# A fixed TensorE order for the first stage of a two-layer backbone, with the spread sums left in PSUM

## The chip, the cores and the metric

The kernel runs on one core of a Trainium2 chip. The metric is the device time of one execution in microseconds; lower is better. A core has five engines with their own instruction queues: TensorE (PE in the profile; PEld is its weight loads), VectorE (DVE), ScalarE (ACT), GpSimd (POOL) and SyncE (SP), which issues the DMAs here. Engines wait for each other through semaphores, each in the order of its own queue.

## The reference

512 latent tokens and 256 context tokens of width 1024 pass through two layers. Each normalizes its tokens, scales and shifts them by a vector computed from a condition, applies a mixer, and adds the result through a gate. The part that matters here is the head of layer 0: the norm, the modulation, and the first product with `w_in`.

```python
D_MODEL, SEQ, CTX_LEN, DEPTH = 1024, 512, 256, 2

def _rms(x):
    xf = x.astype(F32)
    return xf * lax.rsqrt(jnp.mean(xf * xf, axis=-1, keepdims=True) + NORM_EPS)

def modulation(cond, mod_w, mod_b):
    m = jax.nn.silu(cond) @ mod_w + mod_b
    return jnp.split(m, 3, axis=-1)

def trunk_layer(x, ctx, c, c_ctx, mod_w, mod_b, norm_g, mixer, need_ctx_out):
    sh, sc, gt = modulation(c[:, None, :], mod_w, mod_b)
    shc, scc, gtc = modulation(c_ctx, mod_w, mod_b)
    h = rmsnorm(x, norm_g) * (1.0 + sc) + sh
    hc = rmsnorm(ctx, norm_g) * (1.0 + scc) + shc
    y, yc = mixer(h, hc, need_ctx_out)        # layer 0 starts with u = h @ w_in, uc = hc @ w_in
    x = x + gt * y
    if need_ctx_out:
        ctx = ctx + gtc * yc
    return x, ctx
...
    for i in range(DEPTH):                    # layer 0: gated linear recurrence, layer 1: retention
        mod_w, mod_b, norm_g, mixer = layers[i]
        x, ctx = trunk_layer(x, ctx, c, c_ctx, mod_w, mod_b, norm_g, mixer, i < DEPTH - 1)
    return rmsnorm(x, final_norm_g)
```

## The kernel before

All 768 tokens are held transposed: 8 chunks of 128 features on partitions (k = 0 to 7), tokens in the free dimension, 256 context tokens first (`acc_c`), then 512 latent ones (`acc_l`). Each float32 product is three fp32r products: every operand is split into a high part and the rest (`hh`, `hl` for the input, `whi`, `wlo` for the weights), and `mm3` (lines 76 to 78) issues whi x hl, whi x hh and wlo x hh. The tiles of a tile framework are recorded in program order; a scheduler sets the order on each engine, and `tc.issue_after` holds an instruction behind another one. The framework adds the semaphore waits. PSUM is four tiles `slots[0]` to `slots[3]` of 1024 columns.

The first stage, lines 244 to 381, goes from x to the first three column tiles of `h @ w_in`:

- x, 3 MB, comes in eight loads on SP; behind them stand, alternating, tiles of `w_in` (`wraw`, 512 KB) and of the modulation weights (`mraw`, 1 MB for each chunk).
- 48 matmuls of ones (`warm_up`) stand on TensorE while x arrives. ScalarE squares x (lines 306 and 307) and VectorE adds the squares up in `ssum` (line 309).
- `token_sums` (line 198) sums over partitions with six matmuls of one column, line 204 and 205 take square root and reciprocal, `token_spread` (line 209) spreads the result over all partitions with six matmuls, and line 319 copies it to `rstd` in SBUF. `normed(k)` (lines 348 and 349) multiplies a chunk with it: `nx`.
- `mod_mm(f)` (line 328) is the modulation product of a chunk, 16 matmuls of 128 columns; the result is copied to `rows` (line 332). `mod_out(f)` sums it with one selection matmul (line 172) and makes `m` (line 338) and `g` (line 343). The banks are `slots[3][:, 0:512]` and `[:, 512:1024]` in turn.
- `make_h` (lines 223 to 228) scales and shifts `nx` and splits it into `hh` and `hl`.
- For each chunk, `mm_in` then runs three units of six matmuls of 384 columns, one for each weight tile, into slots 0, 1 and 2. The next chunk's modulation product stands ahead of them, its selection matmul behind the first unit.

Behind the stage 16 iterations, the mixer's second half and layer 1 follow; they are not changed.

## Time and profile before

| | us |
|---|---|
| median of 3 runs | 1084.09 |
| lowest, highest | 1082.47, 1084.88 |
| the profiled execution | 1081.4 |
| its span | 1079.6 |
| TensorE busy | 1055.1 (98%) |
| VectorE busy | 707.0 (65%) |
| ScalarE busy | 573.2 (53%) |

The profile is one execution, and its rows are read against its own time. A busy engine at 98% says that little can be hidden and that its idle times are the ones to look for; where they are, the windows and waits by stage say. A matmul in float32 is shown as two, so that a count of x12 stands for six.

### The profile page before, as it was taken

What the parts mean: (1) busy time and instruction counts of PE and PEld (TensorE: products, weight loads), DVE (VectorE), ACT (ScalarE), POOL (GpSimd) and SP (SyncE); (2) the same over time, 40 slices, a digit from 0 to 9 for tenths busy, and PEclk for the clock granted to TensorE, in tenths of its full rate; (3) what the DMA queues carried; (4) which work ended last, traced back from release to release, by engine and by line L of the source; (5) the groups of instructions that cost most, each with busy time, mean ns of one, the idle gap of its engine ahead of it and who ended that gap; (6) DMA issues with size and microseconds to landing.
All of it is one profiled execution on the core that took longest, in us unless ns stands there. A gap on an engine that the chain in (4) does not pass through costs nothing.

```text
span 1079.6 us, 13986 instructions
## 1 busy us (share of the span) xinstructions
PE 1055.1 (98%) x5708; PEld 931.9 (86%) x5708; DVE 707.0 (65%) x991; ACT 573.2 (53%) x745; POOL 1.1 (0%) x5
## 2 busy tenths in 40 slices
PE   8999999999999999999999999999999999999996
PEld 8897879999999999998887778888888888887886
DVE  5776767886688687879989746444554535643356
ACT  6567768767687468788365443123431334322344
POOL 0000000000000000000000000000000000000000
PEclk9999999999999999999999999999999999999998
DMA  9524552221122121222114412212123021220202
GB/s 365 219 88 160 194 176 95 69 85 53 69 69 69 49 69 41 78 77 77 62 40 146 163 43 72 85 39 79 40 78 98 20 78 58 79 99 0 79 1 79
DMA packets 29041, 95.48 MB, mean 88 GB/s; under 512 B 2993, under 2 KB 6193, under 8 KB 27953
## 3 DMA queue, kind: packets, MB, share of 16 engines
q1 hardware_dynamic: 28976, 94.59, 25.3%
q8 instruction: 44, 0.72, 0.3%
q14 instruction: 21, 0.16, 0.0%
HBM read 92.48 MB, written 2.10 MB: 88 GB/s over the span
## 4 chain that ended last, share of the span: by engine, by line
PE 62%; DVE 7%; ACT 7%; issue 2%; DVEq 0%
PE ps L76 21%; PE ps L77 20%; PE ps L78 20%; ACT g L468 1%; ACT a L467 1%; DVE xl L264 1%; DVE g L486 1%; ACT q L470 1%; ACT L483 1%; ACT L467 1%; ACT g L452 1%; DVE wlo L92 1%; DVE q L499 1%; DVE q L492 1%; DVE q L498 1%
## 5 line engine op out<-in xcount | busy, mean ns | idle before, releaser
L76 PE MATMUL ps<-hl,whi 128*128 128x384 f32 (+2 forms) x816 | 286.2, 352 | 1.6 <-DVE hl L228 1.3
L78 PE MATMUL ps<-hh,wlo 128*128 128x384 f32 (+2 forms) x816 | 283.1, 347 | 0.1
L77 PE MATMUL ps<-hh,whi 128*128 128x384 f32 (+2 forms) x816 | 283.0, 347 | 0.0
L91 ACT ACTIVATE whi<-wraw 128x1024 fp32r<-128x1024 f32 (+1 forms) x125 | 125.1, 1002 | 212.8 <-PE ps L77 176.0
L92 DVE TENSOR_TENSOR wlo<-wraw,whi 128x1024 fp32r<-128x1024 f32 (+1 forms) x126 | 145.1, 1153 | 95.5 <-ACT whi L91 79.0
L76 PEld LDWEIGHTS ps<-hl,whi 128*128 128x128 f32 x816 | 153.4, 188 | 20.2 <-issue 4.3
L78 PEld LDWEIGHTS ps<-hh,wlo 128*128 128x128 f32 x816 | 153.4, 188 | 11.0 <-issue 0.8
L77 PEld LDWEIGHTS ps<-hh,whi 128*128 128x128 f32 x816 | 153.5, 188 | 10.2 <-issue 1.0
L76 PE MATMUL ps<-yl,whi 128*128 128x384 f32 (+2 forms) x416 | 142.8, 345 | 3.9 <-DVE yl L501 2.0
L77 PE MATMUL ps<-yh,whi 128*128 128x384 f32 (+2 forms) x416 | 142.2, 342 | 0.0
L78 PE MATMUL ps<-yh,wlo 128*128 128x384 f32 (+2 forms) x416 | 141.2, 342 | 0.0
L76 PEld LDWEIGHTS ps<-yl,whi 128*128 128x128 f32 x416 | 78.0, 188 | 12.8 <-DVE yl L501 2.9
L78 PEld LDWEIGHTS ps<-yh,wlo 128*128 128x128 f32 x416 | 78.2, 188 | 5.5
L77 PEld LDWEIGHTS ps<-yh,whi 128*128 128x128 f32 x416 | 78.2, 188 | 5.0
L76 PE MATMUL ps<-wlo,hh 128*128 128x512 f32 x192 | 75.0, 394 | 1.6 <-DVE rb L673 1.6
L77 PE MATMUL ps<-whi,hh 128*128 128x512 f32 x192 | 74.8, 390 | 0.0
L78 PE MATMUL ps<-whi,hl 128*128 128x512 f32 x192 | 74.3, 389 | 0.0
L452 ACT ACTIVATE g<-ps,vt 128x768 f32<-128x768 f32 x64 | 56.1, 897 | 8.9 <-PE ps L78 8.8
L264 DVE SCALAR_TENSOR_TENSOR xl<-ps,vt,xl 128x255 f32<-128x255 f32 (+1 forms) x96 | 54.3, 605 | 0.0
L630 DVE TENSOR_TENSOR vl<-ps,vh 128x512 fp32r<-128x512 f32 x24 | 16.4, 689 | 49.0 <-ACT vh L629 49.0
L76 PE MATMUL ps<-xlo,whi 128*128 128x384 f32 x128 | 44.5, 349 | 4.0 <-DVE xl L264 2.2
L629 ACT ACTIVATE vh<-ps 128x512 fp32r<-128x512 f32 x24 | 14.1, 598 | 62.0 <-PE ps L78 62.0
(190 smaller groups left out, 1585.6 us busy)
## 6 DMA issues: line engine op xcount, KB each, us to landing
wraw<-in_ret_w_in_dram SPq DMA_DIRECT2D x48, 512.0 KB, 3.5
wraw<-in_lru_w_in_dram SPq DMA_DIRECT2D x32, 512.0 KB, 3.8
mraw<-in_lru_mod_sc_dram SPq DMA_DIRECT2D x8, 1024.0 KB, 10.5
wraw<-in_ret_mod_w_dram SPq DMA_DIRECT2D x16, 512.0 KB, 4.8
wraw<-in_lru_w_out_dram SPq DMA_DIRECT2D x16, 512.0 KB, 3.4
wraw<-in_ret_w_out_dram SPq DMA_DIRECT2D x16, 512.0 KB, 3.9
wraw<-in_lru_w_g_dram SPq DMA_DIRECT2D x16, 256.0 KB, 2.7
wraw<-in_lru_mod_gt_dram SPq DMA_DIRECT2D x8, 512.0 KB, 4.0
```

Source lines behind the costliest of these rows:

```text
L76: nc.tensor.matmul(ps, lhsT=lhs[0], rhs=rhs[1], start=first, stop=False)
L77: nc.tensor.matmul(ps, lhsT=lhs[0], rhs=rhs[0], start=False, stop=False)
L78: return nc.tensor.matmul(ps, lhsT=lhs[1], rhs=rhs[0], start=False, stop=last)
L91: nc.scalar.activation(out=hi, in_=raw, func=AF.Copy)
L92: nc.vector.tensor_tensor(out=lo, in0=raw, in1=hi.bitcast(F32), op=ALU.subtract)
L264: nc.vector.scalar_tensor_tensor(out=t[:, o0:o1], in0=u[:, o0 + sh:o1 + sh], scalar=cw[j], in1=t[:, o0:o1], op0=ALU.mult, op1=ALU.add)
L452: nc.scalar.activation(out=t, in_=ps[:, 128:896], func=AF.Sigmoid, bias=vt[:, boff:boff + 1])
L467: nc.scalar.activation(out=a, in_=r, func=AF.Exp, scale=sneg[:, d * CT + c:d * CT + c + 1])
L468: nc.scalar.activation(out=r, in_=r, func=AF.Tanh, scale=spos[:, d * CT + c:d * CT + c + 1])
L470: nc.scalar.activation(out=q, in_=a, func=AF.Square)
L629: nc.scalar.activation(out=hi, in_=src, func=AF.Copy)
L630: nc.vector.tensor_tensor(out=lo, in0=src, in1=hi.bitcast(F32), op=ALU.subtract)
```

## The change

Loads: the last pair of x loads changes places, the first modulation tile is loaded ahead of the first weights, and four modulation tiles are asked for ahead. The table for the square root is loaded on ScalarE right behind the first activation. The sums: six chunks are squared and added as before, the last two are squared by both engines and go to TensorE as separate matmuls that accumulate in the same six columns, behind a matmul with zeros that opens the accumulation. Square root and reciprocal are taken once for all six columns. The spread is written to `slots[3][:, 256:512]` and `[:, 512:1024]` and read there by `normed`, without the copy to `rstd`; the modulation products use columns 0 to 128 and 128 to 256 of the same slot. The first three weight tiles are split in two parts, the first 128 columns and the rest (`w_part`). Every TensorE instruction of the stage is tied to the one recorded before it (`pin`). From the third chunk on, modulation products stand two chunks ahead of their units.

```diff
-            nc.sync.dma_start(out=acc_c[:, k:k + 2, :], in_=xv[:, k:k + 2, 0:NC])
-            nc.sync.dma_start(out=acc_l[:, k:k + 2, :], in_=xv[:, k:k + 2, NC:NT])
-        nc.scalar.activation(out=cond[:, :, 0:2], in_=vt[:, V_COND:V_COND + 16].rearrange("p (k t) -> p k t", t=2),
+            for a, sl in ((acc_c, slice(0, NC)), (acc_l, slice(NC, NT)))[::-1 if k == 6 else 1]:
+                nc.sync.dma_start(out=a[:, k:k + 2, :], in_=xv[:, k:k + 2, sl])
+        silu = nc.scalar.activation(out=cond[:, :, 0:2], in_=vt[:, V_COND:V_COND + 16].rearrange("p (k t) -> p k t", t=2),
                              func=AF.Silu)
+        with tc.issue_after(silu.ins):
+            nc.scalar.activation(out=warm, in_=eps, func=AF.Sqrt)
...
+            mraw = {0: mod_load(0)}
             fetch_to(0)
-            mraw = {0: mod_load(0)}
-            fetch_to(1)
             mraw[1] = mod_load(1)
             fetch_to(2)
-            mraw[2] = mod_load(2)
+            mraw[2], mraw[3] = mod_load(2), mod_load(3)
...
+            def pin(fn, *args):
+                with ExitStack() as st:
+                    if last_pe[0] is not None:
+                        st.enter_context(tc.issue_after(last_pe[0].ins))
+                    last_pe[0] = fn(*args)
...
-            warm_up(48)
+                    m = nc.tensor.matmul(slots[2][:, 0:P], lhsT=ones, rhs=ones, start=True, stop=True)
+                return m
...
+            def sums_of(parts, first, last):
+                for n, (sq, t) in enumerate(parts):
+                    m = nc.tensor.matmul(tok[:, t:t + 1], lhsT=sq[:, t * P:(t + 1) * P], rhs=ones[:, 0:1], start=False,
+                                         stop=last and n == len(parts) - 1)
+                return m
+
+            tok = slots[1][:, 0:6]
+            none = mp1.tile([P, 6], F32, name="none")
+            nc.vector.memset(none, 0.0)
+            pin(warm_up, 46)
...
-            for k in range(KD):
+            for k in range(6):
...
-            rstd = mp1.tile([P, NT], F32, name="rstd")
-            parts = [(ssum[:, a:b], slots[1][:, 512 * i:512 * i + 4], (slots[0], slots[2])[i][:, 512:512 + b - a], rstd[:, a:b], b - a)
-                     for i, (a, b) in enumerate(segs)]
-            for sq, pt, _, _, n in parts:
-                token_sums(pt, sq, n)
-            warm_up(2)
-            rts = [token_rstd(pt, n, D)[0] for _, pt, _, _, n in parts]
-            for rt, (_, _, ps, rs, n) in zip(rts, parts):
-                spread = token_spread(ps, rt, n)
-                nc.scalar.activation(out=rs, in_=ps, func=AF.Copy)
-
-            bank = [slots[3][:, 0:512], slots[3][:, 512:1024]]
+            sq6, sq7 = e("sq6"), e("sq7")
+            for k, sq in ((6, sq6), (7, sq7)):
+                nc.scalar.activation(out=sq[:, NC:NT], in_=acc_l[:, k, :], func=AF.Square)
+                nc.vector.tensor_tensor(out=sq[:, 0:NC], in0=acc_c[:, k, :], in1=acc_c[:, k, :], op=ALU.mult)
+            nc.vector.tensor_tensor(out=sq6[:, NC:NT], in0=sq6[:, NC:NT], in1=sq7[:, NC:NT], op=ALU.add)
+            pin(lambda: nc.tensor.matmul(tok, lhsT=ones, rhs=none, start=True, stop=False))
+            pin(sums_of, [(ssum, t) for t in range(6)], True, False)
+            pin(sums_of, [(sq, t) for sq in (sq6, sq7) for t in range(2)], False, False)
+            pin(sums_of, [(sq6, t) for t in range(2, 6)], False, True)
+            rt = mp1.tile([P, 6], F32, name="rt6")
+            nc.scalar.activation(out=rt, in_=tok, func=AF.Sqrt, scale=1.0 / D, bias=eps)
+            nc.vector.reciprocal(out=rt, in_=rt)
+            rsp = [slots[3][:, 256:512], slots[3][:, 512:1024]]
...
+                bank = slots[3][:, P * (f % 2):P * (f % 2) + P]
...
+                if f + 4 < KD:
+                    mraw[f + 4] = mod_load(f + 4)
+                rows[f] = mp.tile([P, P], F32, tag="rows", name="rows", bufs=2)
+                nc.scalar.activation(out=rows[f], in_=bank, func=AF.Copy)
+                return m
+
+            def mod_out(f):
+                pt = slots[3][:, P * (f % 2):P * (f % 2) + 4]
...
-                nc.vector.tensor_tensor(out=t[:, 0:NC], in0=acc_c[:, k, :], in1=rstd[:, 0:NC], op=ALU.mult)
-                nc.vector.tensor_tensor(out=t[:, NC:NT], in0=acc_l[:, k, :], in1=rstd[:, NC:NT], op=ALU.mult)
+                nc.vector.tensor_tensor(out=t[:, 0:NC], in0=acc_c[:, k, :], in1=rsp[0], op=ALU.mult)
+                nc.vector.tensor_tensor(out=t[:, NC:NT], in0=acc_l[:, k, :], in1=rsp[1], op=ALU.mult)
...
+            def w_part(i, sl):
+                if i == len(w3):
+                    w3.append((wp.tile([P, 1024], F32R, tag="whi", name="whi"), wp.tile([P, 1024], F32R, tag="wlo", name="wlo")))
+                raw, (hi, lo) = raws[i][0], w3[i]
+                nc.scalar.activation(out=hi[:, sl], in_=raw[:, sl], func=AF.Copy)
+                nc.vector.tensor_tensor(out=lo[:, sl], in0=raw[:, sl], in1=hi[:, sl].bitcast(F32), op=ALU.subtract)
...
+            head, rest = slice(0, P), slice(P, 1024)
+            us[0], gps, us[1] = slots[0], slots[1], slots[2]
+            dst = [us[0], gps, us[1]]
+
+            def unit(k, i):
+                return mm_in(w3[i], dst[i], [k])
...
+            pin(mod_mm, 0)
+            pin(token_spread, rsp[0], rt[:, 0:2], NC)
+            pin(token_spread, rsp[1], rt[:, 2:6], NL)
+            w_part(0, head)
+            nx = normed(0)
+            pin(mod_out, 0)
+            make_hs(0, nx)
+            pin(warm_up, 3)
+            pin(mod_mm, 1)
+            pin(warm_up, 2)
+            with tc.issue_after(last_lo[0].ins):
+                nx = normed(1)
+                w_part(1, head)
+                w_part(0, rest)
+            pin(unit, 0, 0)
+            pin(mod_out, 1)
+            make_hs(1, nx)
+            w_part(2, head)
+            with tc.issue_after(last_lo[0].ins), tc.issue_after(last_hi[0].ins):
+                nx = normed(2)
+                w_part(1, rest)
+                w_part(2, rest)
+            pin(unit, 0, 1)
+            pin(unit, 0, 2)
+            pin(mod_mm, 2)
+            pin(unit, 1, 0)
+            pin(mod_out, 2)
+            make_hs(2, nx)
+            nx = normed(3)
+            pin(unit, 1, 1)
+            pin(unit, 1, 2)
+            pin(mod_mm, 3)
+            pin(unit, 2, 0)
+            pin(mod_out, 3)
+            make_hs(3, nx)
+            nx = normed(4)
+            pin(unit, 2, 1)
+            pin(mod_mm, 4)
+            pin(unit, 2, 2)
+            pin(mod_out, 4)
...
+                if k + 2 < KD:
+                    pin(mod_mm, k + 2)
+                pin(unit, k, 0)
+                if k + 2 < KD:
+                    pin(mod_out, k + 2)
+                    make_hs(k + 2, nx)
                     if k + 3 < KD:
-                        mraw[k + 3] = mod_load(k + 3)
-                    rows = mod_mm(k + 1)
-                    nx = normed(k + 1)
-                mm_in(w3[0], us[0], [k])
-                if k + 1 < KD:
-                    mod_out(k + 1, rows)
-                mm_in(w3[1], gps, [k])
-                mm_in(w3[2], us[1], [k])
+                        nx = normed(k + 3)
+                pin(unit, k, 1)
+                pin(unit, k, 2)
```

On TensorE, from the program's start to the first product: `ones` are warm-up matmuls, `ssum` and `sq` token sums, `rt` the spread, `mraw` a modulation product, `rows` a selection, `ps_67` to `ps_70` slots 0 to 3. Before:

```order
L300 MATMUL ps_69<-ones 128x128 x50
L198 MATMUL ps_68<-ones,ssum 128x1 x6
L209 MATMUL ps_67<-vt,rt 128x128 x2
L209 MATMUL ps_69<-vt,rt 128x128 x4
L328 MATMUL ps_70<-mraw,cond 32x128 x16
L300 MATMUL ps_69<-ones 128x128 x2
L172 MATMUL ps_70<-vt,rows 128x4
```

The same place in the changed program:

```order
L311 MATMUL ps_69<-ones 128x128 x46
L336 MATMUL ps_68<-none,ones 128x6
L316 MATMUL ps_68<-ones,ssum 128x1 x6
L316 MATMUL ps_68<-ones,sq_196 128x1 x2
L316 MATMUL ps_68<-ones,sq_197 128x1 x2
L316 MATMUL ps_68<-ones,sq_196 128x1 x4
L351 MATMUL ps_70<-mraw,cond 32x128 x16
L209 MATMUL ps_70<-vt,rt_218 128x128 x6
L362 MATMUL ps_70<-vt,rows 128x4
```

The modulation product of chunk 0 now stands ahead of the spread, and the spread writes slot 3.

On TensorE, from the last unit of chunk 0 to the first of chunk 1, with the semaphores that an instruction waits for (DMAHW of a load, DVE_49 of VectorE, Activation_49 of ScalarE). Before:

```order
L78 MATMUL ps_69<-hh,wlo 128x384
L328 MATMUL ps_70<-mraw,cond 32x128 [waits DMAHW6_49]
L328 MATMUL ps_70<-mraw,cond 32x128 x15
L76 MATMUL ps_67<-hl,whi 128x384 [waits DVE_49]
L77 MATMUL ps_67<-hh,whi 128x384 [waits Activation_49]
```

The same place in the changed program:

```order
L78 MATMUL ps_69<-hh,wlo 128x384
L351 MATMUL ps_70<-mraw,cond 32x128 [waits DMAHW6_49,DVE_49]
L351 MATMUL ps_70<-mraw,cond 32x128 x15
L76 MATMUL ps_67<-hl,whi 128x384
L77 MATMUL ps_67<-hh,whi 128x384 [waits Activation_49]
```

The wait for VectorE has moved from the unit to the modulation product of chunk 2.

On VectorE, around hl of chunk 1 (`hl`) and nx of chunk 2 (`nx`). Before:

```order
L225 TENSOR_SCALAR tmp<-nx,g_82,m_81 128x256 [waits DVE_49]
L348 TENSOR_TENSOR nx<-acc_c,rstd 128x256
L228 TENSOR_TENSOR hl<-tmp,hh 128x256 [waits DVE_49,Activation_49]
L349 TENSOR_TENSOR nx<-acc_l,rstd 128x512 [waits DMAHW4_49]
L228 TENSOR_TENSOR hl<-tmp,hh 128x512 [waits Activation_49]
L338 TENSOR_TENSOR m_81<-ps_70,vt 128x2x2 [waits PE_49]
```

The same place in the changed program:

```order
L225 TENSOR_SCALAR tmp<-nx,g_82,m_81 128x256 [waits DVE_49]
L228 TENSOR_TENSOR hl<-tmp,hh 128x256 [waits DVE_49,Activation_49]
L228 TENSOR_TENSOR hl<-tmp,hh 128x512 [waits Activation_49]
L374 TENSOR_TENSOR nx<-acc_c,ps_70 128x256 [waits DMAHW3_49]
L375 TENSOR_TENSOR nx<-acc_l,ps_70 128x512
L385 TENSOR_TENSOR wlo<-wraw,whi 128x896 [waits Activation_49] x2
L363 TENSOR_TENSOR m_81<-ps_70,vt 128x2x2 [waits PE_49]
```

nx of chunk 2 has moved behind both parts of hl of chunk 1 and reads slot 3; two weight rests stand between it and m of chunk 2.

## Rows read from the trace of the kernel before

**Rows 1.** the windows by stage; columns: window, its length, busy us of each engine with instructions, granted clock, DMA share, GB/s

```profile
15.50:23.67 8.17, 6.46 (x98) 5.67 (x98) 5.14 (x13) 4.70 (x10) 0.00 (x0) 1.00 1.02 418
23.67:59.70 36.03, 35.00 (x351) 31.26 (x352) 24.85 (x74) 20.32 (x35) 0.00 (x0) 1.00 0.53 203
```

**Rows 2.** the timeline to the first product; start us, us, engine, line, operation, idle before

```profile
13.97 1.17 PE L300 MATMUL ps<-ones 128*128 128x128 f32 x9
...
15.53 1.50 PE L198 MATMUL ps<-ones,ssum 128*128 128x1 f32 x12 [0.38 <-DVE ssum L309]
...
17.58 1.60 PE L209 MATMUL ps<-vt,rt 128*128 128x128 f32 x12 [0.56 <-DVE rt L205]
...
19.11 1.08 PE L328 MATMUL ps<-mraw,cond 128*32 128x128 f32 x32
...
19.85 0.69 DVE L349 TENSOR_TENSOR nx<-acc_l,rstd 128x512 f32<-128x512 f32 x1 [0.68 <-ACT rstd L319]
...
20.26 0.28 ACT L332 ACTIVATE rows<-ps 128x128 f32<-128x128 f32 x1 [0.44 <-PE ps L328]
...
21.01 0.16 DVE L338 TENSOR_TENSOR m<-ps,vt 128x4 f32<-128x4 f32 x1 [0.47 <-PE ps L172]
...
22.93 0.69 DVE L228 TENSOR_TENSOR hl<-tmp,hh 128x512 fp32r<-128x512 f32 x1
...
23.67 0.45 PE L76 MATMUL ps<-hl,whi 128*128 128x384 f32 x1 [1.14 <-DVE hl L228]
```

**Rows 3.** waits of the weight loads, 23.6 to 60 us; waiter, waited for: total, times, longest

```profile
PEld ps L76 <- DVE hl L228: 3.2, 6, 1.4
...
PEld ps L172 <- ACT rows L332: 0.7, 1, 0.7
PEld ps L78 <- DVE wlo L92: 0.6, 2, 0.5
```

**Rows 4.** the timeline from selection matmul to nx, chunks 2 and 5

```profile
30.22 0.28 PE L172 MATMUL ps<-vt,rows 128*128 128x4 f32 x2
...
32.00 0.68 DVE L349 TENSOR_TENSOR nx<-acc_l,rstd 128x512 f32<-128x512 f32 x1
...
43.55 0.38 PE L172 MATMUL ps<-vt,rows 128*128 128x4 f32 x2 [0.40 <-ACT rows L332]
...
45.75 0.68 DVE L349 TENSOR_TENSOR nx<-acc_l,rstd 128x512 f32<-128x512 f32 x1
```

**Rows 5.** the timeline around chunk 1 and the third modulation product

```profile
24.14 1.22 DVE L92 TENSOR_TENSOR wlo<-wraw,whi 128x1024 fp32r<-128x1024 f32 x1
...
25.73 1.31 ACT L223 ACTIVATE hh<-nx,m,g 128x256 fp32r<-128x256 f32 x2 [0.89 <-DVE g L343]
...
26.94 0.80 ACT L227 ACTIVATE tmp<-nx,m,g 128x512 f32<-128x512 f32 x1
...
27.78 1.08 PE L328 MATMUL ps<-mraw,cond 128*32 128x128 f32 x32
```

**Rows 6.** the timeline of one unit between product and selection

```profile
48.15 0.44 PE L76 MATMUL ps<-hl,whi 128*128 128x384 f32 x1
...
49.31 0.28 PE L172 MATMUL ps<-vt,rows 128*128 128x4 f32 x2
```

**Rows 7.** the timeline of VectorE, two 768-column operations with and without a PSUM source

```profile
64.37 0.96 DVE L277 TENSOR_TENSOR sil<-ps,sil 128x768 f32<-128x768 f32 x1
...
68.00 0.96 DVE L271 TENSOR_TENSOR xlo<-xl,xh 128x768 fp32r<-128x768 f32 x1
```

**Rows 8.** TensorE's timeline at two long idle times, and a window at the end

```profile
520.87 0.50 PE L76 MATMUL ps<-yl,whi 128*128 128x512 f32 x1 [1.71 <-DVE yl L501]
...
1070.75 0.61 PE L198 MATMUL ps<-ones,fs 128*128 128x1 f32 x4 [1.96 <-DVE fs L851]
...
1072.00:1074.00 2.00, 1.23 (x4) 0.93 (x4) 0.72 (x2) 0.00 (x0) 0.00 (x0) 0.50 0.87 285
```

**Rows 9.** TensorE's waits from 60 to 480 us

```profile
PE ps L182 <- DMA wraw<-in_ret_mod_w_dram: 1.2, 1, 1.2
```

More of the change, by code (lines that the diff above doesn't have):

```diff
@@ L282, in mm_in @@
                 for a, b in halves:
-                    mm3(ps[:, 128 + a:128 + b], wk, cut(hs[k], a, b), k == 0, k == KD - 1)
+                    m = mm3(ps[:, 128 + a:128 + b], wk, cut(hs[k], a, b), k == 0, k == KD - 1)
+            return m
         with tc.tile_pool(name="mp", bufs=4) as mp, tc.tile_pool(name="mp1", bufs=1) as mp1:
@@ L289, in mod_load @@
                 return t
+            mraw = {0: mod_load(0)}
             fetch_to(0)
-            mraw = {0: mod_load(0)}
-            fetch_to(1)
             mraw[1] = mod_load(1)
             fetch_to(2)
-            mraw[2] = mod_load(2)
+            mraw[2], mraw[3] = mod_load(2), mod_load(3)
+            rows = {}
+            last_pe = [None]
+            def pin(fn, *args):
[3 more added lines that the diff above has]
+                    last_pe[0] = fn(*args)
             def warm_up(n):
                 for _ in range(n):
-                    nc.tensor.matmul(slots[2][:, 0:P], lhsT=ones, rhs=ones, start=True, stop=True)
-            warm_up(48)
+                    m = nc.tensor.matmul(slots[2][:, 0:P], lhsT=ones, rhs=ones, start=True, stop=True)
[9 more added lines that the diff above has]
+            pin(warm_up, 46)
             ssum = e("ssum")
-            for k in range(KD):
+            for k in range(6):
                 sq = ssum if k == 0 else e("sq")
@@ L327, in mod_mm @@
                         j = 2 * s + k % 2
-                        nc.tensor.matmul(bank[f % 2][32 * j:32 * j + 32, 0:P], lhsT=cond[:, k, :],
-                                         rhs=raw[:, (s * KD + k) * P:(s * KD + k + 1) * P],
-                                         start=(k < 2), stop=(k >= KD - 2), tile_position=(0, 32 * j))
-                rows = mp.tile([P, P], F32, tag="rows", name="rows", bufs=2)
-                nc.scalar.activation(out=rows, in_=bank[f % 2][:, 0:P], func=AF.Copy)
-                return rows
-            def mod_out(f, rows):
-                pt = bank[f % 2][:, 128:132]
-                mod_sum(rows, slice(0, P), V_SEL, 4, pt)
+                        m = nc.tensor.matmul(bank[32 * j:32 * j + 32, :], lhsT=cond[:, k, :],
+                                             rhs=raw[:, (s * KD + k) * P:(s * KD + k + 1) * P],
+                                             start=(k < 2), stop=(k >= KD - 2), tile_position=(0, 32 * j))
+                if f + 4 < KD:
+                    mraw[f + 4] = mod_load(f + 4)
+                rows[f] = mp.tile([P, P], F32, tag="rows", name="rows", bufs=2)
+                nc.scalar.activation(out=rows[f], in_=bank, func=AF.Copy)
+                return m
+            def mod_out(f):
+                pt = slots[3][:, P * (f % 2):P * (f % 2) + 4]
+                m = nc.tensor.matmul(pt, lhsT=rows[f], rhs=vt[:, V_SEL:V_SEL + 4], start=True, stop=True)
                 nc.vector.tensor_tensor(
@@ L344, in mod_out, with make_hs @@
                                                scalar2=vt[:, V_LG + f:V_LG + f + 1], op0=ALU.add, op1=ALU.mult)
+                return m
             def normed(k):
                 t = e("nx")
-                nc.vector.tensor_tensor(out=t[:, 0:NC], in0=acc_c[:, k, :], in1=rstd[:, 0:NC], op=ALU.mult)
-                nc.vector.tensor_tensor(out=t[:, NC:NT], in0=acc_l[:, k, :], in1=rstd[:, NC:NT], op=ALU.mult)
-                return t
-            split_to(0)
-            with tc.issue_after(spread.ins):
-                rows = mod_mm(0)
-            mod_out(0, rows)
-            warm_up(4)
-            us[0], gps, us[1] = slots[0], slots[1], slots[2]
-            nx = normed(0)
-            for k in range(KD):
+                nc.vector.tensor_tensor(out=t[:, 0:NC], in0=acc_c[:, k, :], in1=rsp[0], op=ALU.mult)
+                nc.vector.tensor_tensor(out=t[:, NC:NT], in0=acc_l[:, k, :], in1=rsp[1], op=ALU.mult)
+                return t
+            w3 = []
+            def w_part(i, sl):
[4 more added lines that the diff above has]
+                nc.vector.tensor_tensor(out=lo[:, sl], in0=raw[:, sl], in1=hi[:, sl].bitcast(F32), op=ALU.subtract)
+            def make_hs(k, nx):
                 tmp = e("tmp")
@@ L363, in backbone @@
                 make_h(cut(hs[k], NC, NT), NL, nx[:, NC:NT], g0[:, k, 0:1], m0[:, k, 0:1], tmp[:, NC:NT], k == 0)
-                if k == 0:
-                    with tc.issue_after(last_lo[0].ins), tc.issue_after(last_hi[0].ins):
-                        w3 = take(3, 2)
+            head, rest = slice(0, P), slice(P, 1024)
[43 more added lines that the diff above has]
+            pin(mod_out, 4)
+            make_hs(4, nx)
+            nx = normed(5)
+            for k in range(3, KD):
                 if k == 3:
```

4 lines of the change are left out of this document (3 added, 1 removed).

## The prediction

> **What bounds the kernel now.** I read the windows by stage first: from the first product to the end of the first stage (23.67 to 59.70 us) TensorE is busy 35.00 of 36.03 us, at a granted clock of 1.00, while VectorE and ScalarE are far from full [rows 1]. What counts is where TensorE stands still. Then the timeline ahead of the first product, read backwards [rows 2]: the product at 23.67 waited for hl, which hangs on m (21.01), on the modulation product (19.11) and on nx, which ends at 19.85 + 0.69 = 20.54; nx hangs on the spread matmuls (17.58), these on the token sums (15.53). So the chain from x is the bound until 23.67. Last the waits of the weight loads from there to the end of the stage [rows 3]: 3.2 us for hl, of which 1.4 stand ahead of the first product, 0.7 for rows, 0.6 for wlo, together 1.8 + 0.7 + 0.6 = 3.1 us of holes. The whole prize is these 3.1 us and whatever the chain gives ahead of 23.67. Behind the stage the order of every engine is the same in both programs, so a shift of its end shifts the whole.
>
> **The chain, step by step.** *Warm-up and sums.* Nine warm-up passes span 1.17 us from 13.97, so with 0.28 for the last one a pass is issued every 0.11 [rows 2]. The new order has 46 warm-up matmuls before the sums where the old had 50, two passes each: 8 passes or 0.89 us less, so TensorE is free at about 14.98 - 0.89 = 14.09 instead of waiting for ssum until 15.53. But the sums are now 1 + 6 + 4 + 4 = 15 matmuls or 30 passes where they were 12 (1.50 us). 29 x 0.111 + 0.25 = 3.48, so they end at 17.57, against 15.53 + 1.50 = 17.03. Their data are no limit, since the last one is wanted only at 16.6 and the old, longer chain of adds was done at 15.5. **+0.5 us.**
>
> *Modulation product and spread.* The product of chunk 0 now stands ahead of the spread: it starts 0.2 behind the last sum's last pass (17.52) and ends 1.08 later, at 18.60 [rows 2]. Square root and reciprocal run beside it; 17.58 - 17.03 = 0.55 puts them at 18.1. The spread, however, writes columns 256 to 512 of slot 3, and the product and its copy use columns 0 to 128. The built order makes the spread wait for ScalarE, and the value that it waits for is that of the copy to rows. The copy takes 0.28 [rows 2]: 18.60 + 0.07 + 0.28 + 0.05 = 19.00 against 17.58. The copy of the sums to rstd is saved, yet nx now waits for all twelve passes (1.60, so 20.65) and runs 0.33 + 0.69 to 21.67, against 20.54. The selection matmul waits for nx, which reads the same bank: it starts at 21.72, m at 22.14 against 21.01. From m to the first product took 23.67 - 21.01 = 2.66; 0.08 of it goes, since the next nx no longer stands in between. First product at about 24.7: **+1.05 us** instead of a gain. If the first modulation load is late, up to 19.11 - 17.5 = 1.6 is added; I take nothing, because it moves ahead of a 512 KB load, 1.3 us at 418 GB/s [rows 1].
>
> *Reading the sums from PSUM.* No row has nx with such a source. The nearest are two 768-column tensor_tensor, one with a PSUM source and one without, both 0.96 [rows 7]. I take no extra cost; as bounds I put 0 and 0.06 on each of some fourteen reads in the chain, under 1 us.
>
> **The stage.** From chunk 2 on, the product of a chunk waits not only for its load but for VectorE, as the built order shows, and by the value of the wait it is the 512-column nx of the same chunk. Before, nx read rstd from SBUF and nobody waited for it. So each modulation product now stands behind a VectorE chain, and in the pinned order no unit can pass it. A product takes 1.08 [rows 5], a unit of six matmuls 1.16 behind a product (48.15 to 49.31) and 1.04 behind another unit, the selection 0.23 with the slower start behind it [rows 6].
>
> *Chunk 2.* hl of chunk 0 starts at 24.7 - 0.74 = 23.96 (22.93 to 23.67 before [rows 2]). Behind it stand on VectorE its own 0.60, nx(1) with 0.33 + 0.60, a weight head of 128 columns, 0.2, the rest of the first weight, 1.0 (896 columns at the rate of the 1.22 for 1024 [rows 5]), then m, the second head and g, 0.6: tmp and hh of chunk 1 start at 27.3. To the end of tmp it took 26.94 + 0.80 - 25.73 = 2.01 [rows 5]; hl 0.60 and nx(2) 0.33 + 0.69 follow: 30.95, and 0.05 for the wait. TensorE is done with three units and a selection at 24.7 + 0.1 + 3.12 + 0.23 = 28.15. Hole **2.85 us**; the product stands at 31.0 where it stood at 27.78 [rows 5].
>
> *Chunks 3 to 7.* From the selection to the end of the next nx took 32.00 + 0.68 - 30.22 = 2.46 us in an order on VectorE that is kept; with softplus steps between, 45.75 + 0.68 - 43.55 = 2.88 [rows 4]. With 0.05 for the wait, and as cover the selection and the units in between: chunk 3 has two units (0.23 + 2.08), hole 0.2; chunk 4 one, hole 1.25; chunk 5 none, because its product stands right behind the selection of chunk 4, hole 2.4; chunks 6 and 7 have two, and softplus steps, 0.5 each. With chunk 2 that is 2.85 + 0.2 + 1.25 + 2.4 + 0.5 + 0.5 = 7.7 us. The old 3.1 us go, because the hs of a chunk is ready while TensorE stands: 7.7 - 3.1 = **+4.6**.
>
> The weights' split into head and rest is in the VectorE walk above. On SP, each later modulation load still waits for the product that frees its buffer; chunk 2's was there at 27.78 and is wanted later now. The table load for Sqrt moves ahead of the squares, where ScalarE waits for x.
>
> **A rule beside it.** The rows show only that nx held nobody up while it read SBUF. The Trainium skill, "PSUM — Partial Sum Buffer", section "PSUM bank collisions raise a hardware error", says that two engines must not touch the same bank and quadrant at once, even at other columns, and that PSUM is guarded by bank, not by address. It speaks against this change. With that rule the sum is the one here; by address alone it would be that of the third rival.
>
> **Sum.** 1.05 + 4.6 = +5.65 us. The profiled execution took 1081.4 (span 1079.6), so it would take 1087.1; it is one of the quicker ones. On the median of three, 1084.1, I forecast **1089.8 us**.
>
> **Rivals.** *The clock falls in a hole.* Near the end TensorE stood 1.96 us, did a few one-column passes, and from 1072 on had a granted clock of 0.50, the 1.2 GHz level; after 1.71 us at 519 to 521 it went on at full pace [rows 8]. The new holes of 2.85 and 2.4 are longer than both. The Trainium skill, "TensorE: Matmul & The Clock Gate", Part 1, has idle lower the clock to 1.2 GHz and sustained work bring it back; the end of the trace agrees. Price: the work between two holes, some 3 us, at half pace is 3 us more, so 1092.8 with one fall, and some 1094.8 with two, since part of the second hides in the next hole.
>
> *A later stage takes some of it back.* The one long wait behind the stage that hangs on a load is 1.2 us [rows 9]: 1088.6.
>
> *The guard does not bind*, and the holes are those of data alone. Chunk 1's units would wait for hl until 27.3 + 2.01 + 0.69 + 0.1 = 30.1, with TensorE there at 29.3, 0.8; chunk 2's m stands behind two weight rests (2.0), which makes about 1.1 more, wlo 0.3. 1.05 + 2.2 - 3.1 = +0.15: 1084.2.
>
> *Faster.* The pinned order really fills: product beside square root and reciprocal, spread at 18.15, no copy to rstd, the first product 0.4 us sooner, and the 3.1 us of holes gone: 1080.6. It decides if nx of a chunk ends before the unit ahead of its product; 2.46 us against a cover of 0.14 to 2.3 speak against it.
>
> **How the numbers follow.** Forecast 0.62, clock 0.20, taken back 0.06, no guard 0.07, faster 0.05. The range of 1086.6 to 1094.8 takes in the first three; its lower end is the forecast less the 1.2 of rows 9 and 2.0 for the sum of holes and the spread of runs (1082.47 to 1084.88), its upper end two falls. About 0.2% or 2.2 us is what a measurement of this kernel can tell from no change: faster 0.05, same 0.07, slower 0.88.
>
> **What would show it.** In the profile of the changed kernel: the first product at 24.2 to 25.2; among the waits of the modulation product one of about 2.85 us and one of 2.4, both ended by VectorE's nx; windows of the stage at clock 1.00; everything behind it later by the same 5 to 6 us. The prediction is wrong if modulation products start right behind the units, or if the first product comes before 23.7.

## The result

The changed kernel takes 1092.05 us (median of 4 runs, 1091.2 to 1093.17) where the kernel before takes 1083.62 (median of 4, 1082.47 to 1084.88). The ratio is 1.0082, with a 95% interval of 1.007 to 1.0094: slower by 8.4 us. The profiled execution has a span of 1089.4 us against 1079.6, a difference of 9.8; it is 0.9 below its median, the one of before was 2.2 below its own.

Windows of the changed kernel, cut where its stages and its granted clock change; columns as in [rows 1]:

```profile
13.90:16.78 2.88, 2.88 (x28) 2.88 (x27) 1.17 (x3) 0.00 (x0) 0.00 (x0) 0.96 1.02 411
16.78:23.40 6.62, 5.93 (x50) 5.07 (x49) 0.74 (x3) 1.58 (x4) 0.00 (x0) 0.50 1.02 418
23.40:27.19 3.79, 2.81 (x45) 2.31 (x45) 3.11 (x9) 1.98 (x5) 0.00 (x0) 1.00 1.01 419
27.19:33.43 6.24, 3.62 (x21) 3.30 (x21) 5.00 (x13) 3.69 (x5) 0.00 (x0) 1.00 0.60 239
33.43:37.16 3.73, 3.73 (x38) 3.35 (x39) 1.95 (x2) 0.28 (x1) 0.00 (x0) 0.54 0.27 40
...
27.19:70.25 43.06, 36.36 (x352) 33.10 (x353) 27.72 (x80) 22.29 (x37) 0.00 (x0) 0.96 0.38 139
```

Two things are to be seen. The clock is at 0.50, the 1.2 GHz level, twice: from about 16.6 to 23.4, ahead of the first product, and from about 33.7 to 37. And the last row, which holds the same amount of work as the second of [rows 1] (one matmul more, 0.17 us), has 43.06 - 36.36 = 6.70 us of idle TensorE where before had 36.03 - 35.00 = 1.03.

The timeline of TensorE in the changed kernel, from the sums to the modulation product of chunk 7:

```profile
14.07 1.48 PE L316 MATMUL ps<-ones,ssum 128*128 128x1 f32 x12
15.41 2.50 PE L316 MATMUL ps<-ones,sq 128*128 128x1 f32 x16
17.85 1.93 PE L351 MATMUL ps<-mraw,cond 128*32 128x128 f32 x32
20.18 2.93 PE L209 MATMUL ps<-vt,rt 128*128 128x128 f32 x12 [0.40 <-ACT rows L357]
24.21 0.39 PE L362 MATMUL ps<-vt,rows 128*128 128x4 f32 x2 [1.11 <-DVE nx L375]
...
27.19 0.44 PE L76 MATMUL ps<-hl,whi 128*128 128x384 f32 x1 [0.16 <-DVE hl L228]
...
33.43 1.79 PE L351 MATMUL ps<-mraw,cond 128*32 128x128 f32 x32 [2.62 <-DVE nx L375]
...
44.40 1.08 PE L351 MATMUL ps<-mraw,cond 128*32 128x128 f32 x32 [1.08 <-DVE nx L375]
...
49.07 1.08 PE L351 MATMUL ps<-mraw,cond 128*32 128x128 f32 x32 [2.23 <-DVE nx L375]
...
54.22 1.08 PE L351 MATMUL ps<-mraw,cond 128*32 128x128 f32 x32 [0.40 <-DVE nx L375]
...
59.19 1.08 PE L351 MATMUL ps<-mraw,cond 128*32 128x128 f32 x32 [0.33 <-DVE nx L375]
```

The modulation products of chunks 2, 4, 5, 6 and 7 wait for nx of their chunk, which none did before [rows 5]. On VectorE the first of these waits looks like this:

```profile
31.75 0.69 DVE L228 TENSOR_TENSOR hl<-tmp,hh 128x512 fp32r<-128x512 f32 x1 [0.98 <-ACT tmp L227]
32.36 0.41 DVE L374 TENSOR_TENSOR nx<-acc_c,ps 128x256 f32<-128x256 f32 x1
32.69 0.68 DVE L375 TENSOR_TENSOR nx<-acc_l,ps 128x512 f32<-128x512 f32 x1
33.29 1.08 DVE L385 TENSOR_TENSOR wlo<-wraw,whi 128x896 fp32r<-128x896 f32 x1
```

nx of chunk 2 ends at 33.37 and the product starts at 33.43. Reading PSUM costs nx nothing: 0.68 us here, 0.69 from SBUF [rows 2].

The 9.8 us of the two profiles: first product 27.19 - 23.67 = +3.52; idle time of the stage 6.70 - 1.03 = +5.67; busy time 36.36 - 35.00 = +1.36, the half clock from 33.7 to 37 and the one matmul more; together +10.55 at the ends of the two windows. Behind them 1.3 come back, down to +9.22 at the last product (1068.51 and 1077.73): 0.17 is that matmul, and before, TensorE waited 1.2 us there for a load [rows 9]. Its waits from 70 to 184 us in the changed kernel hold no load:

```profile
PE ps L76 <- ACT g L531: 0.9, 1, 0.9
```

0.6 us are added behind the last product.

The windows hold equal amounts of work, but 59.70 is not the end of the stage in the kernel before, as the prediction took it. There hl of chunk 7 ends at 56.87 + 0.69 = 57.56, and the first unit of chunk 7 waits for it:

```profile
56.87 0.69 DVE L228 TENSOR_TENSOR hl<-tmp,hh 128x512 fp32r<-128x512 f32 x1 [0.99 <-ACT tmp L227]
57.61 0.19 PEld L76 LDWEIGHTS ps<-hl,whi 128*128 128x128 f32 x1 [0.21 <-DVE hl L228]
```

The seven matmuls from 56.35 to 57.39 are work of the next column tile that the scheduler had put into this wait. So the last matmul of the stage itself starts at 60.69 and, in the changed kernel, at 69.75, 9.06 later, and the order behind the stage is not quite the same in both programs.

### The profile page after: what moved, and what is told of

It is laid out like the page before. It is cut to its first block, busy times and chain, and to the rows that moved or that the text cites. A ratio compares the mean times of both kernels' runs of the same rounds, so it can differ in the third digit from the quotient of the medians.

```text
span 1089.4 us, 14014 instructions
## 1 busy us (share of the span) xinstructions
PE 1059.7 (97%) x5720; PEld 936.9 (86%) x5720; DVE 706.7 (65%) x995; ACT 572.2 (53%) x744; POOL 1.1 (0%) x5
## 4 chain that ended last, share of the span: by engine, by line
PE 64%; DVE 6%; ACT 6%; issue 2%; DVEq 0%
PE ps L76 22%; PE ps L77 21%; PE ps L78 21%; ACT g L547 1%; ACT a L546 1%; DVE g L565 1%; ACT q L549 1%; DVE xl L266 1%; ACT L562 1%; ACT L546 1%; ACT g L531 1%; DVE q L571 1%; DVE q L578 1%; DVE wlo L92 0%; DVE q L577 0%
## 5 line engine op out<-in xcount | busy, mean ns | idle before, releaser
L91 ACT ACTIVATE whi<-wraw 128x1024 fp32r<-128x1024 f32 (+1 forms) x122 | 121.9, 1001 | 213.5 <-PE ps L77 180.2
L92 DVE TENSOR_TENSOR wlo<-wraw,whi 128x1024 fp32r<-128x1024 f32 (+1 forms) x123 | 141.5, 1152 | 95.8 <-ACT whi L91 79.3
```

What stands on the lines that cost most here:

```text
L91: nc.scalar.activation(out=hi, in_=raw, func=AF.Copy)
L92: nc.vector.tensor_tensor(out=lo, in0=raw, in1=hi.bitcast(F32), op=ALU.subtract)
```

## The experiments

The theory after the result: (1) nx reads slot 3, so all that TensorE writes there waits for VectorE, and this makes the holes; (2) the clock falls ahead of the first product because of what TensorE does there, and again in a hole. Rivals: the fixed order makes the holes; the guard is by bank; the clock falls there in any case. Three groups of kernels ran, each beside the kernel before, whose medians there were 1083.89, 1083.27 and 1083.89 us; each ratio below is to the runs of before of the same group.

### The shared slot

**The sums in PSUM alone, in the kernel before.**

```diff
+            rsp = [slots[3][:, 256:512], slots[3][:, 512:1024]]
-            parts = [(..., (slots[0], slots[2])[i][:, 512:512 + b - a], rstd[:, a:b], b - a)
+            parts = [(..., rsp[i], rstd[:, a:b], b - a)
-                nc.scalar.activation(out=rs, in_=ps, func=AF.Copy)
-            bank = [slots[3][:, 0:512], slots[3][:, 512:1024]]
+            bank = [slots[3][:, 0:P], slots[3][:, P:2 * P]]
-            pt = bank[f % 2][:, 128:132]
+            pt = bank[f % 2][:, 0:4]
             (normed multiplies with rsp in place of rstd)
```

> The kernel before with one part of the change alone: the spread is written to slot 3 and read there by nx, without the copy, and the modulation products use columns 0 to 256 of it. No fixed order, old sums, old loads. Theory (sharing slot 3 costs without the rest of the change): the selection matmul of each chunk now waits for nx of that chunk, which stands behind the product, so hl is late; holes at hl of about 2 us for chunks 1 and 4, 0.3 to 1.1 for the others, first product at about 24.5, end of the stage 5 to 6 us later, time about 1088.5, up to 1090 if the clock falls in a hole. Rival (only the fixed order makes the shared slot costly, since the scheduler moves other work into the waits): within 1.5 us of before.

1092.55 us (4 runs), ratio 1.0089 (1.0073 to 1.0104): this one edit costs as much as the whole change. Waits of TensorE from 13 to 80 us, and the window of the stage:

```profile
PE ps L76 <- DVE hl L228: 5.1, 5, 2.0
PE ps L328 <- DVE nx L349: 1.3, 1, 1.3
```

```profile
24.86:69.40 44.54, 39.49 (x352) 35.87 (x353) 26.55 (x75) 19.95 (x35) 0.00 (x0) 0.90 0.40 152
```

Here the products are written ahead of nx in the program, so it is the selection that stands behind nx, and hl is late, as the theory has it. For chunk 1:

```profile
27.53 0.68 DVE L349 TENSOR_TENSOR nx<-acc_l,ps 128x512 f32<-128x512 f32 x1
...
29.22 0.28 PE L172 MATMUL ps<-vt,rows 128*128 128x4 f32 x2
...
32.79 0.44 PE L76 MATMUL ps<-hl,whi 128*128 128x384 f32 x1 [1.96 <-DVE hl L228]
```

The selection of chunk 1 stands behind all three units of chunk 0; before, it stood behind the first of them, at 24.83. I had the time 4 us too low: idle 44.54 - 39.49 = 5.05 is what the holes make, but the busy time is 39.49 against 35.00, 4.5 us more, nearly all of it half clock, in three stretches (about 24 to 27.3, 34.2 to 37.5 and 51.2 to 54.6 us).

**The changed kernel with the sums copied to SBUF.**

```diff
             pin(token_spread, rsp[1], rt[:, 2:6], NL)
+            rstd = mp1.tile([P, NT], F32, name="rstd")
+            nc.scalar.activation(out=rstd[:, 0:NC], in_=rsp[0], func=AF.Copy)
+            nc.scalar.activation(out=rstd[:, NC:NT], in_=rsp[1], func=AF.Copy)
+            rsp = [rstd[:, 0:NC], rstd[:, NC:NT]]
```

> The changed kernel with one thing more: ScalarE copies the spread sums from slot 3 to SBUF, and nx reads the copy. Theory (the products wait because nx reads slot 3): no modulation product waits for nx any more, the 2.6, 1.1 and 2.2 us waits go, what stays are about 0.9 and 1.2 us at hl of chunks 1 and 2 and two of 0.4 to 0.5, the clock falls once (ahead of the first product) and not again at 33 us; first product at about 27, end of the stage about 5.5 us earlier than in the changed kernel, time about 1086.5. Rival (the holes come from the fixed TensorE order, not from the slot): holes of 2 us or more stay at the same places, with hl as their end, and the time stays within 2 us of 1092.

1085.33 us (10 runs), ratio 1.0012 (1.0002 to 1.0022): 6.7 of the 8.4 us are gone, in the same fixed order. TensorE's waits from 27.1 to 64 us:

```profile
PE ps L76 <- DVE hl L228: 2.1, 3, 1.1
PE ps L362 <- ACT rows L357: 0.3, 1, 0.3
PE ps L351 <- DVE m L363: 0.3, 1, 0.3
```

No product waits for nx, and the clock doesn't fall a second time. The first product stays at 27.20. The same 351 matmuls have 37.20 - 34.90 = 2.30 us of idle time:

```profile
27.20:64.40 37.20, 34.90 (x351) 31.44 (x352) 27.44 (x79) 21.44 (x36) 0.00 (x0) 1.00 0.42 158
```

Its profile is 3.9 us longer than that of before (spans of 1083.5 and 1079.6), the medians differ by 1.4: the profiled run of before is one of its quickest.

**Only the context sums copied.**

```diff
             pin(token_spread, rsp[1], rt[:, 2:6], NL)
+            rstd = mp1.tile([P, NC], F32, name="rstd")
+            nc.scalar.activation(out=rstd, in_=rsp[0], func=AF.Copy)
+            rsp = [rstd, rsp[1]]
```

> Only the 256 context sums are copied to SBUF. The 512 latent sums stay in columns 512 to 1024 of slot 3, the other bank, and the modulation products keep columns 0 to 256 in a bank that VectorE no longer reads. Theory (the guard is on the whole slot of two banks): the holes stay, 2.5 to 3, 1, 2.2 us, all ended by the 512-column nx; time 1091 to 1094. Rival (the guard is by bank, as the prediction took it): the holes at the products go as in the run with all sums in SBUF, time about 1086.5.

1091.9 us (one run). TensorE's timeline at the products of chunks 2, 4 and 5:

```profile
34.08 1.93 PE L351 MATMUL ps<-mraw,cond 128*32 128x128 f32 x32 [2.63 <-DVE nx L375]
...
44.97 1.08 PE L351 MATMUL ps<-mraw,cond 128*32 128x128 f32 x32 [1.08 <-DVE nx L375]
49.64 1.08 PE L351 MATMUL ps<-mraw,cond 128*32 128x128 f32 x32 [2.23 <-DVE nx L375]
```

The holes are those of the changed kernel to 0.01 us, though VectorE now reads only columns 512 to 1024, another bank than the products write. So the wait is on the whole slot of 1024 columns, and the prediction's reason for the wait ("reads the same bank") was wrong; the size of the holes was not. The rule of the Trainium skill, "PSUM — Partial Sum Buffer", section "PSUM bank collisions raise a hardware error", asks for a guard by bank and quadrant: what the program waits for here is coarser than that. Whether less would be safe was not tried.

### The clock ahead of the first product

**The old number of sums.** VectorE adds all eight squares, six matmuls instead of fourteen, 53 warm-up matmuls.

```diff
+            for k in (6, 7):
+                sq = e("sq")
...
+                nc.vector.tensor_tensor(out=ssum, in0=ssum, in1=sq, op=ALU.add)
             pin(sums_of, [(ssum, t) for t in range(6)], True, True)
-            pin(sums_of, [(sq, t) for sq in (sq6, sq7) for t in range(2)], False, False)
-            pin(sums_of, [(sq6, t) for t in range(2, 6)], False, True)
```

> The changed kernel with the sums of before: VectorE adds all eight squares, TensorE does six one-column matmuls behind the opening one (14 passes where there were 30), and 53 warm-up matmuls keep it busy until then. The spread sums stay in slot 3. Theory (the long row of one-column passes lowers the clock ahead of the first product): granted clock 1.00 from 14 us to the first product, first product at about 24.5 instead of 27.2, the holes behind it as before them with the clock fall at 33 us, time about 1089.5, 2.5 below the changed kernel. Rival (the clock falls there whatever the sums are, from the spread's wait or the modulation product): 0.50 from 17 to 23 us again, first product at 27 or later, time about 1092.

1090.57 us (4 runs, 1088.81 to 1092.82), ratio 1.0059 (1.0041 to 1.0077). A miss in its main point: the clock fell here too.

```profile
14.70 0.28 PE L336 MATMUL ps<-none,ones 128*128 128x6 f32 x2
16.75 1.50 PE L316 MATMUL ps<-ones,ssum 128*128 128x1 f32 x12 [1.76 <-DVE ssum L335]
18.18 1.85 PE L349 MATMUL ps<-mraw,cond 128*32 128x128 f32 x32
20.41 2.23 PE L209 MATMUL ps<-vt,rt 128*128 128x128 f32 x12 [0.38 <-ACT rows L355]
```

The dummies ended at 14.9 and the last add came late, so TensorE stood for 1.76 us ahead of the twelve one-column passes; the clock fell at about 18.3 and rose at 21.75. The run mixes two causes and doesn't tell them apart. It does show that the hole ahead of the product of chunk 2 (2.6 us here too) need not lower the clock: the granted clock was 1.00 from 31 to 40 us.

**Dummies of 128 columns among the sums.**

```diff
-            pin(sums_of, [(ssum, t) for t in range(6)], True, False)
+            for n in range(3):
+                pin(sums_of, [(ssum, t) for t in range(2 * n, 2 * n + 2)], True, False)
+                pin(warm_up, 1)
             (and one dummy each behind the pairs of sq6 and sq7)
```

> The changed kernel with six warm-up matmuls of 128 columns put in between the token sums, one behind every second or so; all 30 one-column passes stay. Theory (it is the unbroken row of one-column passes that lowers the clock): the clock stays at 1.00 ahead of the first product, which comes at about 25.9, 1.3 us of dummies later than 24.5 but earlier than 27.2; time about 1091. Rival (30 one-column passes are too many, broken up or not): 0.50 again from about 17 us, first product at 28 to 29, time about 1093.5.

1094.67 us (one run), the rival's: the clock was at 0.50 from about 18.4 to 28.6, and the first product came at 29.30.

**Dummies of 512 columns in their place**, and the sums copied to SBUF as above.

```diff
+            def wide(n):
+                for _ in range(n):
+                    m = nc.tensor.matmul(slots[2][:, 0:512], lhsT=ones, rhs=acc_l[:, 0, :], start=True, stop=True)
+                return m
...
-                pin(warm_up, 1)
+                pin(wide, 1)
```

> The changed kernel with the spread sums copied to SBUF, and six dummy matmuls of 512 float32 columns (two passes each) among the 30 one-column passes, where the run before had dummies of 128 columns. Theory (the clock falls because too few columns stream through TensorE while the sums are made): the granted clock stays at 1.00 to the first product, which comes at about 27.2 because the dummies take some 2.6 us; time about 1087.5. Rival (something else in this stretch lowers it, the one-column passes themselves or the wait for the copy to rows): 0.50 again, first product at 30 or later, time about 1090.5.

1088.41 us (4 runs), ratio 1.0048 (1.0033 to 1.0063). The windows ahead of the first product and behind it:

```profile
14.00:29.75 15.75, 14.03 (x132) 10.10 (x130) 5.28 (x15) 4.43 (x11) 0.00 (x0) 1.00 0.95 388
29.75:72.00 42.25, 39.96 (x381) 36.49 (x382) 32.44 (x87) 25.62 (x40) 0.00 (x0) 1.00 0.44 152
```

The clock never fell in this profile, with all 30 passes of the sums, the product and the spread in the same order, where it fell at about 16.6 in the run with the sums in SBUF and no such dummies: that is what the theory forecast. The spread took 1.60 us instead of 2.93 and the product 1.08 instead of 1.93. The size of the dummies was wrong: two passes of 512 columns took 0.94 us, not 0.43, so six cost 5.6 us, the first product came at 29.75, and the run is no cure.

**Squares, sums and x loads of before**, sums copied to SBUF, 52 dummies.

```diff
             (x loads in the order of before)
-            for k in range(6):
+            for k in range(KD):
...
-            sq6, sq7 = e("sq6"), e("sq7")
...
-            pin(warm_up, 46)
+            pin(warm_up, 52)
```

> The changed kernel with the spread sums copied to SBUF and with the squares, sums and x loads of the kernel before: eight chunks added on VectorE, 14 one-column passes, 52 warm-up matmuls that last until just ahead of them. Theory (the fall ahead of the first product needs a long stretch of little work on TensorE; 14 passes right behind dummies are too short for it): clock 1.00 all the way, first product at about 24.2, end of the stage 2 us behind the kernel before, of which 1.2 is given back at the load near 139 us, time about 1084.7. Rival (the clock falls in this order of product and spread anyway): first product at 26.5 or later, time about 1087.

1085.22 us (10 runs, 1082.03 to 1087.72), ratio 1.0018 (1.0007 to 1.0028): the time is near the theory's, the mechanism was not. The dummies ended at 14.7, the sums waited 1.5 us and started at 16.18, and the clock was at 0.50 from about 18.2 to 21.6. In this group x landed later than in the profile of before: the kernel with the sums in PSUM alone has the same code up to its sums, and they start at 16.39 instead of 15.53 [rows 2]. So the times from the start of the sums to the first product are compared below: 8.14 in before, 9.96 here.

### The chain and the order

**The spread in slots 0 and 2**, on top of the last kernel.

```diff
-            rsp = [slots[3][:, 256:512], slots[3][:, 512:1024]]
+            rsp = [slots[0][:, 512:768], slots[2][:, 512:1024]]
```

> As the run before this one, and the spread is written to slots 0 and 2, which are free then, so that it does not wait for the copy of the product to rows. Theory (the guard of slot 3 costs the chain ahead of the first product about 1.3 us): the spread starts right behind the product, first product at about 22.9, 0.5 to 0.8 ahead of the kernel before, holes of 0.5, 0.2, 1.2, 0.4 and 0.5 us behind it, time about 1084.0, the same as before within 0.1%. Rival (the chain is bound by the modulation product and its rows, not by the spread): first product at about 24.2 and no gain over the run before.

1083.55 us (11 runs), ratio 0.9999 (0.9988 to 1.001): near the theory's time, but the first product, expected at 22.9, came at 25.19, so the nearness is partly luck. The spread starts right behind the product, and sums to first product take 25.19 - 16.37 = 8.82 us, 1.1 less than with the spread in slot 3, though the clock still fell:

```profile
16.37 1.50 PE L316 MATMUL ps<-ones,ssum 128*128 128x1 f32 x12 [1.43 <-DVE ssum L330]
17.80 1.14 PE L344 MATMUL ps<-mraw,cond 128*32 128x128 f32 x32
18.87 2.93 PE L209 MATMUL ps<-vt,rt 128*128 128x128 f32 x12
```

**The same with 59 dummies ahead of the sums.**

```diff
-            pin(warm_up, 52)
+            pin(warm_up, 59)
```

> The kernel of the run with the spread in slots 0 and 2, with 59 warm-up matmuls ahead of the sums where it had 52, so that TensorE doesn't stand for 1.4 us ahead of them; nothing else. Theory (what lowers the clock is the stretch of idle time and one-column passes together, 3.2 us there; without the idle time only the 14 passes are left, as in the kernel before): granted clock 1.00 up to the first product, spread in 1.60 us instead of 2.93, first product 1.9 us earlier, time about 1081.7, 1.5 below the kernel before. Rival (14 one-column passes behind dummies are enough to lower it in this order): 0.50 again from about 18 us, time about 1083.5.

1081.83 us (11 runs), ratio 0.9983 (0.9974 to 0.9992): faster than the kernel before by about 1.8 us, and 0.1 above the 1081.7 that the theory gave. The same place:

```profile
16.77 1.50 PE L316 MATMUL ps<-ones,ssum 128*128 128x1 f32 x12 [0.83 <-DVE ssum L330]
18.20 1.08 PE L344 MATMUL ps<-mraw,cond 128*32 128x128 f32 x32
19.21 1.60 PE L209 MATMUL ps<-vt,rt 128*128 128x128 f32 x12
```

Seven dummies more cut the idle time from 1.43 to 0.83, the spread took 1.60, and sums to first product 23.98 - 16.77 = 7.21 us, 0.9 less than in before. The granted clock was 1.00 from 14 to 62 us. This separates what the run with the old number of sums had mixed: the twelve one-column passes with 1.76, 1.48 and 1.43 us of idle time ahead of them were followed by a fall in all three profiles, with 0.83 us here, and 0.55 and 0.40 in the two kernels below, by none. These are single profiles: other runs of the kernels with 1.48 and 1.43 us had a mean granted clock of 0.998 (1082.03, 1081.86 and 1082.21 us), as high as any here, so it may not have fallen in them.

Where the 1.8 us come from is not traced. The profiled runs of the two kernels took 1081.88 and, before, 1081.4, which is no gain. But 13 of the 33 runs of before in this group had a mean granted clock of 0.993 or 0.994 (1083.28 to 1086.54 us), and none of the 11 here was below 0.996; the 15 runs of before with 0.996 or more have a median of 1082.55. By these times, an estimate, most of the gain goes with a clock that falls less often, and about 0.7 us is left for the shorter chain.

**The weight rests moved** on ScalarE and VectorE, on top of it.

```diff
             (w_hi and w_lo are the two lines of w_part; make_hs calls its third argument between the two parts of hl)
-            make_hs(1, nx)
             w_part(2, head)
-            with tc.issue_after(last_lo[0].ins), tc.issue_after(last_hi[0].ins):
+            w_hi(1, rest)
+            w_hi(2, rest)
+            make_hs(1, nx, lambda: w_lo(1, rest))
+            with tc.issue_after(last_lo[0].ins):
                 nx = normed(2)
-                w_part(1, rest)
-                w_part(2, rest)
...
-            make_hs(2, nx)
+            make_hs(2, nx, lambda: w_lo(2, rest))
```

> As the run before this one, and the rests of the second and third weights are converted earlier: on ScalarE ahead of hh of chunk 1, on VectorE between the two parts of hl of chunk 1 and of chunk 2, so that they don't stand ahead of m of chunk 2. Theory (the 1.1 us hole at hl of chunk 2 comes from the two weight rests on VectorE): that hole goes, some 0.6 us come back at hl of chunk 1 and 0.3 to 0.9 at wlo, stage end 0.5 us earlier, time 0.3 to 0.5 below the run before. Rival: the holes only change places, no gain.

1081.93 us (11 runs), ratio 0.9987 (0.9978 to 0.9996): no gain over the run before. The 1.1 us hole at hl of chunk 2 went, the 0.6 at hl of chunk 1 stayed, and a new one of 0.6 came at wlo; what was left of the gain doesn't show in the time.

**Without the fixed order**, first in the kernel of 59 dummies, then in the changed kernel.

```diff
             def pin(fn, *args):
                 with ExitStack() as st:
-                    if last_pe[0] is not None:
-                        st.enter_context(tc.issue_after(last_pe[0].ins))
                     last_pe[0] = fn(*args)
```

> As the first run of this group (spread in slots 0 and 2, sums in SBUF, 59 dummies), without the fixed order: each TensorE instruction stands where the scheduler puts it. Theory (with the slot free the order matters little): the scheduler puts the product of chunk 2 behind the first matmul of its unit and leaves a hole of 1.7 us at hl of chunk 1, and the 1.2 us hole of chunk 2 goes; time within 1 us of the first run, rather 0.6 below it. Rival (the fixed order is worth something by itself): 1 us or more slower than the first run.

1081.88 us (10 runs), ratio 0.9984 (0.9973 to 0.9994), 0.05 from the pinned one: with the slot free the fixed order is worth nothing that shows.

> The changed kernel without the fixed order alone: sums stay in slot 3, 30 passes. Theory (the wait for nx in slot 3 is in the data, the order only decides what can stand in it): the scheduler fills part of the holes, stage end about 2 us earlier than in the changed kernel, the clock falls ahead of the first product as there, time about 1090. Rival (the fixed order makes the loss): time below 1086.

1087.94 us (10 runs), ratio 1.0043 (1.0025 to 1.0061), between the two theories: 4 us below the changed kernel. For the same 351 matmuls TensorE has 39.15 - 37.65 = 1.50 us of idle time, against 6.70 with the fixed order:

```profile
30.58:69.73 39.15, 37.65 (x351) 34.10 (x352) 27.40 (x79) 21.97 (x36) 0.00 (x0) 0.92 0.38 140
```

One product still waits for nx, 0.7 us. So in the changed kernel the holes need both, the shared slot and the fixed order: without the first 2.30 us of idle time are left, without the second 1.50. The order doesn't make the wait, but it keeps other work out of it; the rival was half right. The shared slot alone can cost as much in another order, as its run in the kernel before shows (5.05). What this profile, of one of the longest runs, pays is the clock: 37.65 us of busy time, and the first product at 30.58. The ten runs go from 1084.58 to 1092.44, and their mean granted clock goes with them: 0.996 to 0.998 in the three shortest, 0.988 to 0.990 in the four longest. One program is spread over 8 us, and the clock is what differs.

## Why the prediction was right, and where it was off

The measured 1092.05 lies in the range of 1086.6 to 1094.8, 2.3 above the forecast of 1089.8. The sign and the mechanism of the stage were right: two of the signs that were named, a long wait for nx at chunk 2 and one at chunk 5, came. The others did not: the first product at 24.2 to 25.2, a clock of 1.00 in the stage, and a shift of 5 to 6 us. What came is nearest to the first rival, the clock, at 1092.8 for one fall; but there were two falls, one where the rival didn't look for it, and each cost less than its 3 us, so that the nearness of this number is luck.

- **The chain at full clock**: forecast 24.7, measured 27.19. The clock's part is 2.5: sums to product 17.85 - 14.07 = 3.78 against the forecast 3.43; product to spread 2.33 against 1.47 with 512-column dummies; spread to first product 7.01 against 5.70 there (the copy to SBUF in that run doesn't make the difference: 7.02 in the run with the copy alone). 27.19 - 0.35 - 0.86 - 1.31 = 24.67, so the chain's own +1.05 holds, and 30 passes, the wait for the copy to rows and the twelve passes of the spread were sized right.
- **The place of the fall**: the rival looked for it in the holes behind the first product. It came ahead of it, in a stretch without any hole: from 13.90 to 16.78 TensorE is busy 2.88 of 2.88 us, nearly all of it one-column passes. [rows 2] had 12 of them, and 12 became 28, behind two of six columns; I counted the 2 us more as time on the path and not as something the clock could answer to.
- **The holes**: forecast 2.85, 0.2, 1.25, 2.4, 0.5 and 0.5, together 7.7; measured 2.62, under 0.2, 1.08, 2.23, 0.40 and 0.33, 6.7 us of idle time in all. Places, releaser and sizes were right.
- **The subtraction** is the step that failed in the forecast itself: the 3.1 us of old holes are waits of the weight loads [rows 3], the new ones were worked out as idle time of TensorE. In that measure the old holes are 1.03 us [rows 1]. 6.70 - 1.03 = 5.67 instead of 4.6; with like from like the forecast would have been 7.7 - 1.03 + 1.05 = 7.7, about 1091.8.
- **A fall in a hole**: one, behind the 2.62; 3.87 us from the product to the next unit (33.43 to 37.30) against 2.35 in chunk 3, so 1.5 and not 3. None behind the 2.23, the clock is at 1.00 from 37.2 on.
- **A later stage takes some back**: 1.2, as the second rival had it, at the load that [rows 9] names. The prediction's sentence that the order behind the stage is the same in both programs was not quite right (the seven matmuls above), which changes nothing in the sum.
- **The guard does not bind** and **the pinned order fills**: ruled out by the holes; the runs with the sums in SBUF show that both come near once the slot is free.

What stays open: whether the clock falls behind a given stretch. It fell behind a hole of 2.6 us in the changed kernel and not in the run with six sums; one program has it fall in some runs and not in others.

## What to carry to other kernels

Before an operand is left in PSUM to save a copy, list who writes the same slot: here each of them waited for every reader, and in a fixed order nothing else could fill the wait; the copy gave back 6.7 of 8.4 us. Take old and new holes from the same view, idle time of the engine or waits of its loads, before one is subtracted from the other. And count a stretch of one-column matmuls ahead of the main loop as a risk to the clock, not only as time: here seven dummies ahead of it made the median 1.7 us shorter.

## What the runs showed of the hardware that was not expected

The granted clock fell at about 16.6 us, 2.5 us into a row of 28 one-column passes, without idle time on TensorE. With six float32 dummies of 128 columns among them it fell too (0.50 from 18.4 us), with six of 512 columns it did not (1.00 throughout). The Trainium skill, "TensorE: Matmul & The Clock Gate", Part 1, has the clock depend on how busy TensorE has been and names idle as what lowers it; the trace shows a fall without idle time, so an engine that the profile calls busy is not safe from it. A dummy of 512 float32 columns took 0.94 us, 0.47 a pass, a pass of 128 columns or of one 0.11.
